# A hybrid gMLP and SSD streaming step on one core: the queues' order from the list schedule over the timeline model

## The chip, the cores and the metric

The kernel runs on one core of one Trainium2 chip. A core has five engines with a queue of instructions each: TensorE (PE, products), VectorE (DVE), ScalarE (ACT), GpSimd (POOL) and SyncE (SP, which here only issues DMAs). An engine takes its queue from the front; a semaphore makes it wait for another engine or for a DMA. The metric is the device time of one execution in microseconds (us), the median of several runs.

## The reference

One layer. The rows of a prompt of 4096 tokens and of a sample of 64 tokens are normalised, multiplied by one input projection, sent through two mixers and through one output projection:

```python
h = rms_norm(x, norm_in_w) @ w_in            # (tokens, 1024) @ (1024, 5648)
u, v, g, z, xbc, dt_raw = jnp.split(h, SPLITS, axis=-1)
a_out, vn = gmlp_branch(u, v, g, ...)        # (u * (W_s LN(v) + b)) * silu(g), chunks of 128
b_out, h_last, new_conv = mamba_branch(z, xbc, dt_raw, ...)  # conv, silu, SSD scan, norm(y * silu(z))
y = x + jnp.concatenate([a_out, b_out], axis=-1) @ w_out
y_prompt = rms_norm(yp, norm_f_w)
```

It returns both outputs, the final states of scan and convolution, and the normalised rows `vn` of the sample. All is float32.

## The kernel before, in words

**Number format.** A float32 operand of a large product is split into a high part (a cast to the format that TensorE takes, on ScalarE) and a low part (operand minus high part, on VectorE or GpSimd). Each product is then three: high by high, low by high, high by low. A matmul therefore waits for a cast and for a subtraction.

**Stages.** The 32 chunks of 128 tokens are cut into five blocks of 6 chunks and a last block of 2 chunks with the sample. For each block the rows are read, normalised and turned over (`xrows`: norm L481 on VectorE, transposes L488 on TensorE, copies L491 on ScalarE), and `right_operands` makes seven Strassen operands of them, called `hop1` to `hop7`: sums L524, L527, L530 and L533 (the second and third on VectorE, L533 on GpSimd), high parts L514 on ScalarE, low parts L515. Their products come in the order 1, 2, 4, 6, 7, 5, 3. The first columns of a block are the gMLP's values (`v_stage`, matmuls L1083 to L1085), the rest come by units of columns (`products`, matmuls L1123 to L1125, twelve for one weight tile). `add_up` (L1136 to L1153) adds the seven products out of PSUM. Convolution is at L1165 to L1186, the gate by z at L1223 to L1239 (its multiplication is `z_fin`, L1230 on VectorE).

**The weight operands.** In block 0 every weight operand is made on the chip, by `make`: sums of raw weights into `wx` tiles (L386, L401, L403, L405, mostly GpSimd), the cast L392 on ScalarE into a `w` tile, and the subtraction L393:

```python
src = r[{1: "a11", 2: "a12", 4: "a22", 6: "a11", 7: "a22", 5: "a21", 3: "a12"}[q]]
act.copy(hi, src)
(pool if q in self.on_pool[u[0]] else dve).tensor_tensor(lo, src, hi.bitcast(F32), SUB)
```

It is also stored to DRAM, and the later blocks load it from there (SP's queue). There are four `w` tiles; a load or a cast into one waits for the matmuls that read its contents before. The last block loads most operands and casts some (L358).

**The scan.** A unit of the scan is one chunk and one of two groups of heads. It loads running decay values (`acb`, DMA at L823), makes decays (`ssd_decay`, L864 to L869: two exponentials `ea` L869 on ScalarE), a masked matrix (`ssd_m`: eight L882 and one L885 on ScalarE, then L890 on VectorE), turns x over (L897) and scales it (`xdt` L907), multiplies (`ssd_y`: eight matmuls L928, four L931) and updates the state (L978 to L989). Units of one block are worked off between the products of the same block. ScalarE loads a table when the next function is not in the table that it holds; such loads stand in its queue as instructions of their own.

**Phase 2** multiplies the mixed rows by `w_out`: casts and subtractions L1582/L1583 for the weights and L1590/L1591 for the rows, matmuls L1628 to L1630, sums L1643/L1645, store L1650.

**What sets the order.** The source issues the instructions of all stages in one text order. The framework records them; at the end its list schedule makes the five queues: it keeps, for a modelled machine, when each engine is free and when each instruction's inputs are there, and puts next, of the instructions that are ready, the one that stood earliest in the text. An engine can so get later text first, wherever the model thinks that the earlier text is not ready. Order on a queue, semaphores, and the places of table loads follow from that.

## Time and profile before

| what | us |
|---|---|
| median of 3 runs | 2957.86 (2954.97 to 2960.79) |
| the profiled execution, its own time | 2957.03 |
| its span in the trace | 2955.1 |
| granted TensorE clock, mean | 0.982 of full speed |
| block 0 | 0 to 521 |
| blocks 1 to 4 | 521 to 2085, 391 each |
| last block and start of phase 2 | 2085 to 2320 |
| phase 2 | 2320 to 2955 |

The profile gives, for each engine, busy time and the idle time before its instructions with what ended it. Times in its rows are us from the start of the span unless marked ns. A line number names the place in the kernel's text. Tile names carry no number in the profile and carry one in the order of the instructions.

### The profile page before, as it was taken

What the parts mean: (1) busy time and instruction counts of PE and PEld (TensorE: products, weight loads), DVE (VectorE), ACT (ScalarE), POOL (GpSimd) and SP (SyncE); (2) the same over time, 40 slices, a digit from 0 to 9 for tenths busy, and PEclk for the clock granted to TensorE, in tenths of its full rate; (3) what the DMA queues carried; (4) which work ended last, traced back from release to release, by engine and by line L of the source; (5) the groups of instructions that cost most, each with busy time, mean ns of one, the idle gap of its engine ahead of it and who ended that gap; (6) DMA issues with size and microseconds to landing.
All of it is one profiled execution on the core that took longest, in us unless ns stands there. A gap on an engine that the chain in (4) does not pass through costs nothing. (4 is left out here: it accounts for less than half of the span.)

```text
span 2955.1 us, 46403 instructions
## 1 busy us (share of the span) xinstructions
PE 2826.3 (96%) x17159; PEld 2633.3 (89%) x17159; DVE 2162.7 (73%) x3607; ACT 1345.8 (46%) x2655; POOL 704.8 (24%) x575
## 2 busy tenths in 40 slices
PE   5988988999999999999999999999999899999998
PEld 5987887999999999999999999999899688878886
DVE  7888887667756777676677576874666766698887
ACT  4366655145643266541565514663365222253332
POOL 4554443110012100031000221000301433353332
PEclk8999998999999999999999999999999899999999
DMA  6666777777787777886777877778777555454553
GB/s 223 252 233 237 258 281 261 245 229 238 248 277 270 229 238 243 270 288 227 244 241 240 300 264 229 234 246 281 241 251 226 168 171 171 159 169 157 171 171 111
DMA packets 306809, 679.14 MB, mean 230 GB/s; under 512 B 30472, under 2 KB 154072, under 8 KB 306584
## 3 DMA queue, kind: packets, MB, share of 16 engines
q1 hardware_dynamic: 305544, 676.17, 68.6%
q8 instruction: 137, 2.24, 0.3%
q14 instruction: 88, 0.72, 0.1%
q10 hardware_dynamic: 1040, 0.00, 0.0%
HBM read 525.34 MB, written 150.75 MB: 229 GB/s over the span
## 5 line engine op out<-in xcount | busy, mean ns | idle before, releaser
L1123 PE MATMUL mm<-hop,w 128*128 128x384 f32 x1656 | 579.4, 350 | 7.1 <-ACT w L392 3.5
L1125 PE MATMUL mm<-hop,w 128*128 128x384 f32 x1656 | 564.9, 341 | 9.0 <-DVE w L393 4.5
L1124 PE MATMUL mm<-hop,w 128*128 128x384 f32 x1656 | 565.0, 341 | 0.0
L1629 PE MATMUL pa<-wlo,oh 128*128 128x512 f32 (+1 forms) x928 | 366.7, 395 | 13.0 <-DVE wlo L1583 13.0
L1630 PE MATMUL pa<-whi,ol 128*128 128x512 f32 (+1 forms) x928 | 364.9, 393 | 3.5 <-DVE ol L1591 3.5
L1628 PE MATMUL pa<-whi,oh 128*128 128x512 f32 (+1 forms) x928 | 365.2, 394 | 2.6 <-ACT whi L1582 1.4
L1123 PEld LDWEIGHTS mm<-hop,w 128*128 128x128 f32 x1656 | 315.4, 190 | 14.0 <-ACT w L392 7.0
L1125 PEld LDWEIGHTS mm<-hop,w 128*128 128x128 f32 x1656 | 315.3, 190 | 12.2 <-DVE w L393 7.0
L1124 PEld LDWEIGHTS mm<-hop,w 128*128 128x128 f32 x1656 | 315.5, 190 | 3.4 <-issue 2.4
L1123 PE MATMUL mm<-hop,wy 128*128 128x384 f32 x864 | 297.4, 344 | 0.0
L1125 PE MATMUL mm<-hop,wy 128*128 128x384 f32 x864 | 292.0, 338 | 0.0
L1124 PE MATMUL mm<-hop,wy 128*128 128x384 f32 x864 | 291.9, 338 | 0.0
L1629 PEld LDWEIGHTS pa<-wlo,oh 128*128 128x128 f32 (+1 forms) x928 | 174.6, 188 | 57.1 <-DVE wlo L1583 18.9
L1630 PEld LDWEIGHTS pa<-whi,ol 128*128 128x128 f32 (+1 forms) x928 | 174.8, 188 | 42.7 <-DVE ol L1591 4.2
L1628 PEld LDWEIGHTS pa<-whi,oh 128*128 128x128 f32 (+1 forms) x928 | 174.5, 188 | 42.5 <-ACT whi L1582 2.1
L123 POOL TENSOR_TENSOR rsx<-rsx,mhalf 128x1 f32<-128x1 f32 (+1 forms) x33 | 19.0, 588 | 736.6 <-DVE rsx L122 736.6
L1083 PE MATMUL mm<-w,hop 128*128 128x260 f32 x552 | 160.4, 291 | 16.2 <-ACT hop L514 16.2
L1085 PE MATMUL mm<-w,hop 128*128 128x260 f32 x552 | 159.6, 290 | 7.7 <-DVE hop L515 7.7
L882 ACT ACTIVATE acb<-acb,acu 128x128 f32<-128x128 f32 (+1 forms) x528 | 166.6, 389 | 0.6
L1124 PEld LDWEIGHTS mm<-hop,wy 128*128 128x128 f32 x864 | 162.6, 188 | 0.7
L1123 PEld LDWEIGHTS mm<-hop,wy 128*128 128x128 f32 x864 | 162.5, 188 | 0.8
L1125 PEld LDWEIGHTS mm<-hop,wy 128*128 128x128 f32 x864 | 162.3, 188 | 0.0
(333 smaller groups left out, 6517.8 us busy)
## 6 DMA issues: line engine op xcount, KB each, us to landing
w<-wop_c SPq DMA_DIRECT2D x114, 512.0 KB, 4.3
w<-wop_v SPq DMA_DIRECT2D x84, 520.0 KB, 5.0
w<-wop_u SPq DMA_DIRECT2D x76, 512.0 KB, 4.3
w<-wop_g SPq DMA_DIRECT2D x76, 512.0 KB, 4.4
w<-wop_z SPq DMA_DIRECT2D x76, 512.0 KB, 4.6
wy<-wop_c SPq DMA_DIRECT2D x72, 512.0 KB, 4.4
acb<-acd SPq DMA_DIRECT2D x66, 512.0 KB, 5.1
raw<-ab SPq DMA_DIRECT2D x64, 512.0 KB, 4.1
```

The source lines that it names most:

```text
L123: pool.tensor_tensor(out, out, mhalf[: out.shape[0]].to_broadcast(list(out.shape)), ALU.pow)
L882: act.activation(M[:L, i, :L], M[:L, i, :L], AF.Relu, bias=self.acu[:L, ci, h0 + i : h0 + i + 1])
L1083: pe.matmul(pv, a, hi[:, j, :], start=(j == 0), stop=False)
L1085: pe.matmul(pv, b, hi[:, j, :], start=False, stop=(j == 3))
L1123: pe.matmul(b, hi[:, j, :], thi[:, j, :], start=j == 0, stop=False)
L1124: pe.matmul(b, hi[:, j, :], tlo[:, j, :], start=False, stop=False)
L1125: pe.matmul(b, lo[:, j, :], thi[:, j, :], start=False, stop=j == 3)
L1628: pe.matmul(b, x[0][:, j, :], hi, start=first, stop=False)
L1629: pe.matmul(b, x[0][:, j, :], lo, start=False, stop=False)
L1630: pe.matmul(b, x[1][:, j, :], hi, start=False, stop=last)
```

## The change

One argument is added where the kernel's context is opened. The text of the kernel is the same, and so are its instructions, apart from ScalarE's table loads (116 in place of 106) and semaphores.

```diff
-    with _tile.TileContext(nc) as tc:
+    with _tile.TileContext(nc, schedule_with_timeline_sim=True) as tc:
         hybrid_step_kernel(tc, *args)
```

With it the list schedule goes by another machine model, the framework's timeline model, when it asks which instructions are ready. The rule, earliest text first, stays. On TensorE 11,583 of 15,979 instructions keep their place against the others, on VectorE 1,583 of 3,608, on ScalarE 1,006 of 2,485, on GpSimd 462 of 573. Three places show how.

ScalarE in block 0, before: `w_1812` to `w_1856` are weight operands, `ea_2265` belongs to unit 0 of the scan; the eight L882 of unit 0 come only behind these rows.

```order
L392 CAST w_1812<-wx_1449 128x512
L1186 ACT_TABLE_LOAD
L1186 ACTIVATE arena_155<-arena_155 128x768
L392 CAST w_1835<-wx_1627 128x512
L866 ACT_TABLE_LOAD
L866 ACTIVATE dte_2261<-dte_2261 128x16
L1186 ACT_TABLE_LOAD
L1186 ACTIVATE arena_155<-arena_155 128x768
L392 CAST w_1856<-wx_1816 128x512
L392 CAST w_1877<-wx_1816 128x512
```

The same place now; ahead of these rows stand already both L869 of units 0 and 1 (`ea_2265`, `ea_2354`) and the eight L882 of unit 0 (`acb_2252`).

```order
L866 ACTIVATE dte_2350<-dte_2350 128x16
L392 CAST w_1812<-wx_1449 128x512
L882 ACTIVATE acb_2259<-acb_2259,acu_311 128x128 x6
L392 CAST w_1835<-wx_1627 128x512
L882 ACTIVATE acb_2259<-acb_2259,acu_311 128x128 x2
L885 ACTIVATE acb_2252<-acb_2252 128x1024
L1186 ACT_TABLE_LOAD
L1186 ACTIVATE arena_155<-arena_155 128x768
L885 ACT_TABLE_LOAD
L885 ACTIVATE acb_2259<-acb_2259 128x1024
L848 COPY bt_2306<-ss_2254 128x256
L392 CAST w_1856<-wx_1816 128x512
```

The scan's exponentials and masks of two units now stand ahead of the casts `w_1812` to `w_1856`; before they stood behind them, in pieces.

TensorE in block 0, at the first L928; `hop6_151` and the like are the Strassen operands of the rows, `ss` and `mm` PSUM banks. Before:

```order
L1125 MATMUL mm_2358<-hop6_151,w_2222 128x384
L1123 MATMUL mm_2397<-hop7_152,w_2245 128x384
L928 MATMUL ss_2336<-acb_2252,xdt_2308 64x128 x8
L931 MATMUL ss_2345<-arena_155,S_147 128x128 x4
L897 MATMUL ss_2391<-ident_66,arena_155 128x128 x4
L1124 MATMUL mm_2397<-hop7_152,w_2245 128x384
L1125 MATMUL mm_2397<-hop7_152,w_2245 128x384
```

Now:

```order
L1125 MATMUL mm_2058<-hop3_154,w_1986 128x384
L928 MATMUL ss_2336<-acb_2252,xdt_2308 64x128 x8
L931 MATMUL ss_2345<-arena_155,S_147 128x128 x4
L1123 MATMUL mm_2080<-hop1_148,w_2007 128x384
L1124 MATMUL mm_2080<-hop1_148,w_2007 128x384
L1123 MATMUL mm_2101<-hop2_149,w_2028 128x384
L1124 MATMUL mm_2101<-hop2_149,w_2028 128x384
L1125 MATMUL mm_2080<-hop1_148,w_2007 128x384
```

Before, the scan's first products stood behind the products with `w_2222`; now they stand behind those with `w_1986`, eleven weight operands earlier, and the four L897 that followed them stand elsewhere. The products with `hop1` and `hop2` are interleaved at their start.

VectorE between two blocks (here from block 1 to block 2): L1230 is the gate of the old block, L515, L527 and L530 make the Strassen operands of the new one. Before:

```order
L1230 TENSOR_TENSOR arena_155<-arena_155 128x768
L1150 TENSOR_TENSOR arena_155<-mm_8751,arena_155 128x3x128
L1151 TENSOR_TENSOR arena_155<-mm_8751,arena_155 128x3x128
L515 TENSOR_TENSOR hop5_153<-t1_8475,hop5_153 128x768
L527 TENSOR_TENSOR arena_155<-arena_155,t1_8475 128x2x384
L527 TENSOR_TENSOR arena_155<-arena_155,t1_8476 128x2x384
L1153 TENSOR_TENSOR arena_155<-mm_8779,arena_155 128x3x128
L1153 TENSOR_TENSOR arena_155<-mm_8800,arena_155 128x3x128
L515 TENSOR_TENSOR hop4_150<-arena_155,hop4_150 128x768
L515 TENSOR_TENSOR hop6_151<-arena_155,hop6_151 128x768
```

Now:

```order
L515 TENSOR_TENSOR hop5_153<-t1_8475,hop5_153 128x768
L515 TENSOR_TENSOR hop5_153<-t1_8476,hop5_153 128x768
L1153 TENSOR_TENSOR arena_155<-mm_8779,arena_155 128x3x128
L1230 TENSOR_TENSOR arena_155<-arena_155 128x768
L1153 TENSOR_TENSOR arena_155<-mm_8800,arena_155 128x3x128
L1230 TENSOR_TENSOR arena_155<-arena_155 128x768
L527 TENSOR_TENSOR arena_155<-arena_155,t1_8475 128x2x384
L530 TENSOR_TENSOR arena_155<-arena_155 128x2x384
L527 TENSOR_TENSOR arena_155<-arena_155,t1_8476 128x2x384
L530 TENSOR_TENSOR arena_155<-arena_155 128x2x384
L1230 TENSOR_TENSOR arena_155<-arena_155 128x768
L515 TENSOR_TENSOR hop3_154<-arena_155,hop3_154 128x768 x2
```

Two L1230 and the second L515 of `hop5` now stand ahead of the first L527; L515 of `hop4`, which stood right behind L527 and L1153, now comes after `hop3`, `hop6` and half of `hop7`. The same move recurs at each of the later boundaries.

## Rows read from the trace of the kernel before

**Rows 1.** the page's first part: engine, busy us, share of the span, instructions

```profile
PE 2826.3 (96%) x17159; PEld 2633.3 (89%) x17159; DVE 2162.7 (73%) x3607; ACT 1345.8 (46%) x2655; POOL 704.8 (24%) x575
```

**Rows 2.** busy time by stretch: length, engines, granted clock, DMA share, GB/s

```profile
0.00:521.00 521.00, 440.22 (x2696) 415.44 (x2696) 424.26 (x632) 290.28 (x563) 251.45 (x187) 0.93 0.71 249
521.00:912.00 391.00, 385.44 (x2545) 375.96 (x2546) 270.91 (x482) 184.04 (x378) 36.39 (x45) 0.99 0.76 250
2085.00:2320.00 235.00, 218.48 (x1442) 200.98 (x1440) 157.63 (x366) 121.67 (x254) 55.13 (x38) 0.96 0.73 236
2320.00:2955.00 635.00, 615.79 (x2684) 500.39 (x2682) 489.28 (x670) 198.41 (x346) 226.99 (x167) 0.99 0.48 159
176.00:264.00 88.00, 74.38 (x403) 68.45 (x401) 70.47 (x87) 58.29 (x99) 50.55 (x43) 0.92 0.68 239
```

**Rows 3.** TensorE's waits in block 0: us in total, times, longest

```profile
PE mm L1083 <- ACT hop L514: 16.2, 2, 15.0
PE ss L928 <- issue: 10.9, 3, 4.9
...
PE ss L488 <- DVE xt L481: 7.7, 4, 4.0
PE ss L928 <- DVE acb L890: 5.3, 2, 4.7
```

**Rows 4.** TensorE's waits in the stretch 176 to 264 us alone

```profile
PE ss L928 <- issue: 4.2, 1, 4.2
PE mm L1125 <- POOL w L393: 4.0, 2, 3.6
PE mm L1123 <- ACT w L392: 2.6, 2, 1.7
```

**Rows 5.** groups on ScalarE, 176 to 264 us: busy, mean ns | idle before

```profile
L392 ACT CAST w<-wx 128x512 fp32r<-128x512 f32 x28 | 16.5, 612 | 15.9 <-POOL wx L405 12.6 <-DMA wx<-in_w_in_dram 1.2 <-POOL wx L401 1.1
L882 ACT ACTIVATE acb<-acb,acu 128x128 f32<-128x128 f32 x22 | 7.4, 392 | 0.1
...
L869 ACT ACTIVATE ea<-acb 64x512 f32<-64x512 f32 x6 | 3.8, 629 | 1.7 <-DVE arena L970 1.1 <-DMA acb<-acd 0.6
...
L885 ACT ACT_TABLE_LOAD x2 | 2.6, 1283 | 0.0
L885 ACT ACTIVATE acb<-acb 128x1024 f32<-128x1024 f32 x2 | 2.1, 1057 | 0.0
```

**Rows 6.** TensorE's waits in blocks 1 to 4 and the last block's start

```profile
PE ss L488 <- DVE xt L481: 7.5, 10, 1.6
```

**Rows 7.** VectorE in order of time, block 1 to 2: start, us, operation

```profile
902.76 0.95 DVE L1230 TENSOR_TENSOR arena<-arena 128x768 f32<-128x768 f32 x1
...
905.43 1.82 DVE L527 TENSOR_TENSOR arena<-arena,t 128x768 f32<-128x768 f32 x2
...
909.85 4.46 DVE L515 TENSOR_TENSOR hop<-arena,hop 128x768 fp32r<-128x768 f32 x4 [1.40 <-ACT hop L514]
914.23 1.81 DVE L530 TENSOR_TENSOR arena<-arena 128x768 f32<-128x768 f32 x2
```

**Rows 8.** TensorE in order of time: the third value product begins

```profile
916.38 0.28 PE L1083 MATMUL mm<-w,hop 128*128 128x260 f32 x1
```

**Rows 9.** groups on ScalarE in the last block, 2140 to 2245 us

```profile
L358 ACT CAST w<-wa 128x512 fp32r<-128x512 f32 x12 | 7.4, 613 | 7.4 <-issue 6.6 <-PE mm L1405 0.7
...
L1417 ACT COPY cvr<-mm 128x256 f32<-128x256 f32 (+1 forms) x16 | 3.8, 292 | 4.1 <-PE mm L1405 4.1
```

**Rows 10.** TensorE's waits in the same stretch of the last block

```profile
PE mm L1403 <- DMA w<-wop_c: 1.4, 1, 1.4
```

**Rows 11.** TensorE's waits in phase 2, 2320 us to the end

```profile
PE pa L1629 <- DVE wlo L1583: 5.9, 5, 2.3
PE pa L1630 <- DVE ol L1591: 3.5, 1, 3.5
```

## Prediction

> **What bounds the kernel now.** I read the page's first part, then the busy times by stretch, then TensorE's waits stretch by stretch. TensorE is busy 96% of the span [rows 1]: 2826.3 of 2955.1 us, so 129 us are idle. A new order of the same instructions can win nothing but idle time and slow clock. The stretches [rows 2] say where that is. Blocks 1 to 4 are nearly full (385.4 of 391 us in block 1). Block 0 is not: it lasts 521 us, TensorE is busy 440.2 of them, and the granted clock is 0.93. It does the work of a later block and makes the weight operands besides; VectorE is busy 424.3 us there, ScalarE 290.3, GpSimd 251.5. So 81 of the 129 idle us lie in block 0, 16.5 in the last block and the start of phase 2, 19.2 in phase 2, and some 12 in all of blocks 1 to 4. The forecast is therefore mostly one on block 0.
>
> TensorE's waits in block 0 [rows 3] are four kinds that count: 15.0 us once for the cast L514 of the fourth operand at the start, 10.9 and 5.3 us for the scan's products L928, and 7.7 us for the transposes L488. The rest are waits for weights, of a few us each. In the stretch 176 to 264 us [rows 4] the weights' part (4.0 for the low part, 2.6 for the cast) stands beside one L928 wait of 4.2 us. A wait of this length costs more than itself: in the 5 us behind that one the granted clock is 0.50 in the last line of [rows 2], the lower of the two levels, 1.2 GHz, so 5.0 us are spent on 2.5 us of work.
>
> The sum is made against the profiled execution, 2957.0 us with a span of 2955.1; the median of the runs is 2957.9, 0.9 us above, which I neglect.
>
> **Block 0, 176 to 264 us.** ScalarE's order puts the exponentials and masks of the scan's first two units ahead of the casts from `w_1812` on. Newly ahead of `w_1856` stand three L869 at 629 ns, sixteen L882 at 392, two L885 at 1057 and one table load at 1283 [rows 5]: 1.9 + 6.3 + 2.1 + 1.3 = 11.6 us. ScalarE's casts stand idle 15.9 us in the 88 us of this stretch, mostly until GpSimd's sums L405 are made [rows 5]; about a fifth of that, 2.8 us, lies ahead of `w_1856`, and takes up so much. The cast then comes some 8.8 us later, and queued behind it are the next casts, the evacuations L1136 and L1175 of the convolution, and through them VectorE's subtractions L393. TensorE, which had the cast just in time before, would wait up to 8.8 us. But a wait here lets GpSimd and VectorE run ahead, so that the later waits of 4.0 and 2.6 us [rows 4] are covered by it: net +2.2 us, to which I add 1.5 for the slower clock behind a longer wait, about +3.7. On the other side, TensorE's first L928 stand eleven weight operands earlier, and their inputs are ready by then: the 4.2 us wait and the 2.5 us lost at half clock behind it go, −6.7. Sum −3. The bounds: −13 if all three waits of rows 4 go with the slow clock (4.2 + 4.0 + 2.6 + 2.5), +9 if the 8.8 us stay whole and nothing is covered.
>
> On the table loads, rows 5 show 1283 ns each, and no idle time between a load and the L885 behind it (0.0). The Trainium skill, "ScalarE: Activation LUTs", section "What ACT_TABLE_LOAD costs", has about 1380 ns of drain on top, 2.66 us for a switch. By the page the ten loads more would put 27 us on ScalarE in place of 12.8, and the four ahead of `w_1856` would make it 5.5 us later still; the row decides, and shows no drain.
>
> The ten loads by the row are 12.8 us on an engine that is busy 46% [rows 1]. They cost nothing of their own where ScalarE waits anyhow; where it doesn't, they are in the 11.6 us above.
>
> **Later in block 0.** Of the other L928 waits 12.0 us are left (10.9 + 5.3 − 4.2, three long ones). In the new order some six matmuls of a product stand ahead of them; in the stretch 247 to 252 us thirty matmuls take 5.0 us at half clock [rows 2], so six take 0.5 us at full clock and 1.0 at half. Three times 1.0: −3 (0 to −12, the latter if VectorE's L890 comes early as well). The transposes L488 stand 36 to 47 matmuls later, that is 3 to 8 us by the same rate, against a longest wait of 4.0 [rows 3]. What would be late next is L491 and, behind it, the operands of block 1, which have no wait of their own before. I take −5 of the 7.7 (0 to −7.7).
>
> **Start of block 0.** L514 of `hop4` stands behind those of `hop7`, `hop5` and `hop6` in both orders, so the 15.0 us [rows 3] stay. Two casts of weights stand newly ahead of it, 0.6 us each by rows 5, and the normalisations of later rows come earlier on VectorE: 0, between −2 and +2.
>
> **Blocks 1 to 4.** Two things move against each other. The L488 waits, 7.5 us in ten places [rows 6], shrink as in block 0, since the transposes stand later: −5. At the boundary VectorE's two gates L1230 and a split of `hop5` now stand ahead of the first L527. One L1230 takes 0.95, an L527 0.91 (two in 1.82), a split 1.1 (four in 4.46) [rows 7]: the sums for `hop4` start three times about 0.95 later, and wait for ScalarE's gate besides; splits of `hop3`, `hop6` and `hop7` go ahead of that of `hop4`, some 4.5 to 5.5 us more. Before, the splits of `hop4` and `hop6` ended at 914.3 (909.85 + 4.46), and the third product began at 916.4 [rows 8]: 2.1 us of cover. TensorE takes the sixth and seventh operands ahead of the rest of the fourth now, each product about 4 us long, which makes up for most of the later split. Left is a wait of about 1.4 us, four times: +5.6 (0 to +7 each if no other product covers, that is +28 at the most). Together about +0.5.
>
> In the fourth convolution unit of each block two L869 and four L882 stand ahead of an evacuation: 2 × 0.63 + 4 × 0.39 = 2.8 us later [rows 5]. PSUM has three further banks, so TensorE feels only what is over: 0 to 2.8, I take 0.5, four times: +2.
>
> **Last block.** Two units of the scan stand ahead of casts L358 (12 of 613 ns) and evacuations L1417 (16 of 292 ns) [rows 9]; each unit is 2 L869, 8 L882, 1 L885 and a table load, 6.7 us by rows 5. TensorE waits only 1.4 us in this stretch [rows 10], so its cover is unknown. Bounds: 0, and the 13.4 us of both units. The casts show 7.4 us of idle time before them, so half of 13.4 is taken up, and a part by banks: +3.
>
> **Phase 2.** The steady part has the same order on TensorE. The 3.5 us wait on L1591 [rows 11] has its row split ahead of a weight's now; the 5.9 us on L1583 stay. −1 (−4 to +3).
>
> **Sum.** −3 −3 −5 +0 +0.5 +2 +3 −1 = −6.5; 2957.0 − 6.5 = 2950.5, say 2951.
>
> **The rivals.**
> *Weights starve TensorE in block 0 (slower).* The place is ScalarE's queue from `w_1812` on. For it: the casts were just in time, ScalarE is busy 58.3 of the 88 us, VectorE 70.5, GpSimd 50.6 [rows 2], so a delay is made good slowly; and the pattern returns with the other units. Against it: 12.6 us of the casts' idle time were spent on GpSimd, which the scan's work on ScalarE could fill. Price: 8.8 us whole, some 4 us at each of three later pairs of units, and 2.5 us of slow clock behind each of the four: 8.8 + 12 + 10 = +31; less the −11 of the other terms, about +20: 2977. It decides where the delay per pair of units is over 5 us.
>
> The Trainium skill, "PSUM — Partial Sum Buffer", section "Engine vs sequencer instructions", calls ScalarE's queue a strict FIFO: no ready cast passes a unit of the scan, which is what this rival needs; of the size of the delay it says nothing.
>
> *Block 0 gains as a whole (faster by more).* If scan products and transposes are ready wherever they now stand, all of 16.2 us (L928) and 7.7 (L488) go, with 2.5 us of slow clock behind each of the three longest: −31, less +8 for the last block, the boundaries and the units: about 2934. For it: TensorE idles 81 us in block 0. Against it: VectorE is busy 81% of the block, and what L928 waits for passes through it.
>
> *Nothing moves in time.* If VectorE sets block 0's pace, the waits only change their names: 2957, ±4. For it: 424 of 521 us busy. Blocks 1 to 4 have no more than 12 us to give or lose before. That the switch does nothing at all is excluded by the order.
>
> **How the numbers follow.** Forecast 0.40 (2943 to 2958), starved weights 0.24 (2967 to 2987), larger gain 0.18 (2925 to 2943), nothing 0.18. A measurement of this kernel can tell about 0.2%, 6 us, from no change; the forecast's 6.5 us lies at that edge, so it splits: 0.23 faster, 0.15 same, 0.02 slower. With the larger gain, faster is 0.41; same 0.15 + 0.16 = 0.31; slower 0.24 + 0.02 + 0.02 = 0.28. The forecast's own range is 2943 to 2958. The range that leaves out 2 in 10 takes in most of both other cases: 2928 to 2982.
>
> **What would show it.** Right: TensorE's waits for L928 in block 0 fall from 16.2 us to about 9, those for L488 in blocks 0 to 4 from 15 to about 5; waits for `w` L392/L393 between 176 and 264 us grow by 2 to 4 us; block 0 ends 8 to 14 us earlier, and the later blocks are no shorter. Wrong: block 0 ends later than 521 us with waits for `w` over 20 us; or a wait for L515 of `hop4` or `hop6` of over 3 us at each boundary; or a wait for L358 or L1417 of over 8 us in the last block.

## The result, and the profile after

The changed kernel takes 3003.41 us (median of 4 runs, 3000.88 to 3007.13) against 2956.41 us for the kernel before in the same comparison: a ratio of 1.0158, with a 95% interval of 1.0140 to 1.0175. It is slower by 47 us. The prediction was 2951 us, with its widest range from 2928 to 2982; the result lies above all of them. The profiled execution has a span of 3005.4 us and a mean granted clock of 0.979.

The first part of the page of the changed kernel, in the columns of [rows 1]:

```profile
PE 2843.8 (95%) x17159; PEld 2636.7 (88%) x17159; DVE 2185.3 (73%) x3607; ACT 1359.5 (45%) x2665; POOL 718.4 (24%) x575
```

TensorE is busy 17 us longer, and its idle time has grown from 129 to 162 us. Some 9 of the 17 us go with the mean granted clock, 0.979 in place of 0.982 (an estimate: 2826.3 us times their ratio).

Busy time by stretch, as in [rows 2]; the first seven lines are block 0, blocks 1 to 4, the last block with the start of phase 2, and phase 2, each cut where the same instructions stand as in the kernel before, and the last line is the stretch of block 0 on which the prediction rested:

```profile
0.00:531.00 531.00, 440.43 (x2704) 408.60 (x2704) 443.77 (x636) 292.55 (x570) 259.41 (x188) 0.94 0.71 249
531.00:927.00 396.00, 389.93 (x2573) 380.72 (x2573) 269.89 (x486) 185.57 (x379) 36.81 (x42) 0.99 0.75 246
927.00:1324.00 397.00, 390.65 (x2575) 381.67 (x2576) 273.51 (x485) 188.36 (x383) 47.61 (x49) 0.99 0.75 248
1324.00:1729.00 405.00, 394.84 (x2604) 384.96 (x2602) 281.36 (x489) 192.68 (x388) 55.06 (x54) 0.99 0.76 248
1729.00:2127.00 398.00, 392.38 (x2585) 382.52 (x2585) 262.55 (x480) 172.56 (x344) 35.86 (x42) 0.99 0.73 239
2127.00:2374.00 247.00, 222.58 (x1445) 201.66 (x1444) 162.26 (x372) 122.61 (x255) 52.67 (x36) 0.97 0.68 221
2374.00:3005.00 631.00, 612.95 (x2680) 496.58 (x2678) 491.98 (x664) 205.19 (x347) 231.00 (x169) 0.99 0.49 160
176.00:264.00 88.00, 71.00 (x369) 65.21 (x369) 72.49 (x84) 57.16 (x98) 48.45 (x38) 0.92 0.60 210
```

Block 0 has grown by 10 us, blocks 1 to 4 by 5, 6, 14 and 7, the last block's stretch by 12; phase 2 got 4 back. Blocks 1 to 4, of which the prediction said that they had no more than 12 us to give or lose, have lost the most.

TensorE's waits over the whole of the changed kernel (us in total, times, longest), to be held against [rows 3, 6, 10, 11]:

```profile
PE mm L1083 <- ACT hop L514: 27.8, 5, 19.8
PE mm L1125 <- DVE w L393: 15.3, 11, 4.2
PE mm L1123 <- DVE cvr L1153: 13.7, 4, 3.5
...
PE mm L1123 <- ACT w L392: 8.3, 6, 4.2
...
PE ss L488 <- DVE xt L481: 7.4, 4, 2.5
PE mm L1403 <- DMA w<-wop_u: 6.5, 4, 2.5
PE mm L1083 <- DVE arena L1138: 6.1, 2, 3.4
PE pst L978 <- DVE xdt L944: 5.9, 3, 3.5
```

The long waits for L928 (16.2 us in block 0) are all but gone, as are those of L488 in blocks 1 to 4. In their place stand four waits of L1123 for L1153 and two of L1083 for L1138, which the kernel before did not have at all, more waits for weights (L393, L392), and longer ones for L514 at the start and the block boundaries.

**Where the time went, counted on the same instructions.** Since the instructions are the same, each of TensorE's can be looked up in both traces. The table gives the median of (start after minus start before) for those that started within 4 us of the named time in the kernel before, and cuts the span at 640, 860, 1030, 1250, 1420, 1640, 1812, 2037, 2320 us, and 2940 near the end. "Block 0" is all up to 640 us, with the boundary behind it. "Units" is the sum of the four differences 640 to 860, 1030 to 1250, 1420 to 1640 and 1812 to 2037, which hold the fourth convolution unit of each block and a part of the block's middle; "boundaries" is what lies between these.

| run | block 0 | units | boundaries | last block | phase 2 | at the end |
|---|---|---|---|---|---|---|
| the change | 10.4 | 22.1 | 9.4 | 12.1 | -3.8 | 50.2 |
| units_back | 8.7 | -1.7 | 7.8 | 10.4 | -4.8 | 20.4 |
| l1175_first | 9.7 | 7.8 | 12.4 | 13.3 | -5.2 | 38.0 |
| l1175_early | 10.3 | -0.7 | 16.2 | 13.3 | -6.4 | 32.7 |
| bounds_back | 10.6 | 16.4 | 6.3 | 13.6 | -3.3 | 43.6 |
| l533_dve | 5.8 | 19.5 | 20.5 | 11.7 | -3.7 | 53.8 |
| block0_back | 3.1 | 21.1 | 10.0 | 9.2 | -6.0 | 37.4 |
| block0_act_back | -2.6 | 22.1 | 5.6 | 8.3 | -5.6 | 27.8 |
| last_back | 9.6 | 18.3 | 9.1 | 1.9 | -1.2 | 37.7 |
| last_act_back | 7.5 | 19.8 | 5.8 | 9.2 | -3.1 | 39.2 |
| last_sp_back | 10.0 | 20.1 | 11.0 | 7.7 | 0.6 | 49.4 |
| last_actsp_back | 7.8 | 22.6 | 13.9 | 1.7 | 0.5 | 46.5 |
| last_rest_back | 8.5 | 18.3 | 9.1 | 19.5 | -1.2 | 54.2 |
| most_back | 2.4 | -1.4 | 5.5 | -0.9 | 0.4 | 5.9 |
| units_only | -0.6 | 7.3 | -0.3 | 5.6 | -1.7 | 10.3 |
| units_act_alone | 2.6 | 24.2 | -0.6 | 1.5 | -0.5 | 27.2 |
| gains | -8.9 | -0.9 | 6.3 | 4.1 | -2.1 | -1.5 |
| gains_b0 | -9.0 | 0.2 | 0.0 | 1.3 | -2.4 | -9.9 |
| gains_b0act | -4.2 | 1.1 | -1.5 | 3.9 | -1.6 | -2.3 |

At 860, 1250 and 1640 us the shift is not steady: in the changed kernel it falls from 15.3 us at 830 to 10.3 at 912, from 22.7 at 1200 to 17.7 at 1303 and from 30.3 at 1560 to 26.8 at 1697. Cut where it is steady and where both kernels have started the same matmuls, by line, tiles and count (518, 640, 830, 912, 1030, 1200, 1303, 1420, 1560, 1697, 1812 and 2037 us), the same traces give:

| run | block 0 to 518 | first boundary | units | middles | three boundaries |
|---|---|---|---|---|---|
| the change | 3.0 | 7.5 | 27.9 | -13.5 | 17.0 |
| units_back | 1.7 | 7.3 | 4.0 | -13.4 | 15.5 |
| l1175_first | 2.5 | 7.3 | 13.7 | -13.6 | 20.1 |
| l1175_early | 2.9 | 7.5 | 5.1 | -13.4 | 23.8 |
| bounds_back | 3.3 | 7.7 | 22.4 | 0.0 | 0.4 |
| l533_dve | 0.6 | 5.7 | 25.4 | -13.5 | 28.2 |
| block0_back | 3.1 | -0.1 | 27.0 | -13.4 | 17.5 |
| block0_act_back | -5.6 | 3.5 | 28.2 | -13.6 | 13.0 |
| last_act_back | 1.6 | 6.1 | 25.7 | -13.5 | 13.4 |
| last_actsp_back | 1.7 | 6.2 | 28.5 | -13.6 | 21.6 |
| most_back | 2.7 | 0.2 | 4.2 | -0.2 | 0.0 |
| units_act_alone | 2.3 | 0.2 | 23.3 | -0.5 | 0.8 |
| gains | -7.3 | -1.5 | 4.8 | 0.7 | 0.0 |
| gains_b0 | -5.9 | -3.0 | -0.2 | -0.1 | 0.5 |

The new order gains 13.5 us in the stretches ahead of the three boundaries, in every run that has it there, and pays 13 to 24 us at the boundaries. One middle in both kernels, with the same 447 matmuls:

```profile
830.00:909.30 79.30, 75.96 (x447) 73.51 (x447) 43.20 (x72) 39.61 (x89) 15.88 (x14) 1.00 0.89 297
```

```profile
845.30:919.60 74.30, 74.30 (x447) 73.74 (x446) 42.70 (x73) 39.65 (x89) 13.27 (x11) 1.00 0.91 316
```

One trace has noise. Between runs with the same order in a stretch, block 0 in the first table came out between 5.8 and 10.6 us, the units of the second between 22.4 and 28.5, the three boundaries between 13.0 and 23.8 (in the first table 5.6 to 16.2), and last block and phase 2 together between 2.7 and 10.3.

**The fourth convolution unit, the largest part.** ScalarE in order of time, in block 1 of the changed kernel (start, us, operation, idle time before it and what ended it):

```profile
642.63 1.28 ACT L869 ACT_TABLE_LOAD   x1
648.46 1.29 ACT L869 ACTIVATE ea<-acb 64x512 f32<-64x512 f32 x2 [4.55 <-DMA acb<-acd]
...
663.92 1.28 ACT L885 ACT_TABLE_LOAD   x1
665.22 1.06 ACT L885 ACTIVATE acb<-acb 128x1024 f32<-128x1024 f32 x1
666.18 1.01 ACT L1175 ACTIVATE arena<-cvr,prm 128x768 f32<-128x768 f32 x1
```

VectorE and TensorE behind it:

```profile
667.29 1.02 DVE L1178 SCALAR_TENSOR_TENSOR arena<-cvr,prm,arena 128x768 f32<-128x768 f32 x1 [9.21 <-ACT arena L1175]
668.23 0.55 DVE L1153 TENSOR_TENSOR cvr<-mm,cvr 128x384 f32<-128x384 f32 x1
```

```profile
668.84 0.44 PE L1123 MATMUL mm<-hop,w 128*128 128x384 f32 x1 [3.40 <-DVE cvr L1153]
```

The chain is read backwards. TensorE's L1123 stands still for 3.40 us, because the PSUM bank it writes to is freed by L1153 on VectorE. L1153 is ready; it stands in VectorE's queue behind L1178, and L1178 waits 9.21 us for ScalarE's L1175. L1175 in turn is ready, but stands in ScalarE's queue behind two units of the scan: a table load at 642.63, then 4.55 us of nothing until the unit's `acb` has come by DMA, then L869, L882 and L885 of both units up to 666.18. In the kernel before, the same L1178 and L1153:

```profile
649.07 1.02 DVE L1178 SCALAR_TENSOR_TENSOR arena<-cvr,prm,arena 128x768 f32<-128x768 f32 x1 [1.47 <-ACT arena L1175]
650.00 0.55 DVE L1153 TENSOR_TENSOR cvr<-mm,cvr 128x384 f32<-128x384 f32 x1
```

There L1178 waited 1.47 us, and TensorE did not wait. The same happens four times, and costs more than the wait where the clock falls behind it:

```profile
668.00:673.00 5.00, 4.17 (x23) 4.17 (x24) 4.96 (x7) 3.52 (x4) 1.73 (x2) 1.00 0.26 67
1065.00:1070.00 5.00, 5.00 (x17) 5.00 (x17) 4.88 (x7) 3.17 (x5) 1.10 (x3) 0.50 0.16 26
```

In block 1 the granted clock stayed at 1.00 behind the wait of 3.40 us, and the shift grew by 3.7 us from 640 to 680 us; in block 2, behind a wait of 3.3 us, it is 0.50 for the next five (1.2 GHz), and the shift grew by 6.2 us from 1030 to 1070. In block 3, behind a wait of 3.5 us, the clock is 0.57 over 1465 to 1470, in block 4 it is 0.83 over 1867 to 1872.

### The profile page after: what moved, and what is told of

Its sections match the earlier page's. It is cut to its first block, busy times and chain, and to the rows that moved or that the text cites. A ratio compares the mean times of both kernels' runs of the same rounds, so it can differ in the third digit from the quotient of the medians.

```text
span 3005.4 us, 46472 instructions
## 1 busy us (share of the span) xinstructions
PE 2843.8 (95%) x17159; PEld 2636.7 (88%) x17159; DVE 2185.3 (73%) x3607; ACT 1359.5 (45%) x2665; POOL 718.4 (24%) x575
## 4 chain that ended last, share of the span: by engine, by line
PE 72%; DVE 10%; ACT 7%; DMA 6%; issue 4%; POOL 1%; SPq 1%; POOLq 0%; ACTq 0%; DVEq 0%
PE mm L1123 11%; PE mm L1125 11%; PE mm L1124 11%; PE pa L1630 6%; PE pa L1629 6%; PE pa L1628 6%; PE mm L1085 2%; PE ss L931 2%; PE ss L928 2%; PE mm L1084 2%; PE mm L1083 2%; ACT acb L882 2%; PE ss L761 2%; DMA wx<-in_w_in_dram 1%; DMA acb<-acd 1%
## 5 line engine op out<-in xcount | busy, mean ns | idle before, releaser
L1123 PE MATMUL mm<-hop,w 128*128 128x384 f32 x1656 | 580.1, 350 | 28.0 <-DVE cvr L1153 13.7
L1125 PE MATMUL mm<-hop,w 128*128 128x384 f32 x1656 | 567.1, 344 | 17.8 <-DVE w L393 15.3
L1123 PEld LDWEIGHTS mm<-hop,w 128*128 128x128 f32 x1656 | 316.2, 191 | 37.2 <-DVE cvr L1153 15.0
L1123 PE MATMUL mm<-hop,wy 128*128 128x384 f32 x864 | 296.8, 344 | 0.6 <-ACT cvr L1136 0.6
L123 POOL TENSOR_TENSOR rsx<-rsx,mhalf 128x1 f32<-128x1 f32 (+1 forms) x33 | 21.1, 640 | 752.2 <-DVE rsx L122 751.1
L1083 PE MATMUL mm<-w,hop 128*128 128x260 f32 x552 | 162.4, 297 | 33.9 <-ACT hop L514 27.8
L1123 PEld LDWEIGHTS mm<-hop,wy 128*128 128x128 f32 x864 | 162.9, 188 | 1.7 <-ACT cvr L1136 0.9
L1085 PE MATMUL mm<-w,hop 128*128 128x260 f32 x552 | 159.1, 292 | 5.3 <-DVE hop L515 5.3
L882 ACT ACTIVATE acb<-acb,acu 128x128 f32<-128x128 f32 (+1 forms) x528 | 162.9, 387 | 0.8
```

The source lines that it names most:

```text
L882: act.activation(M[:L, i, :L], M[:L, i, :L], AF.Relu, bias=self.acu[:L, ci, h0 + i : h0 + i + 1])
L1083: pe.matmul(pv, a, hi[:, j, :], start=(j == 0), stop=False)
L1085: pe.matmul(pv, b, hi[:, j, :], start=False, stop=(j == 3))
L1123: pe.matmul(b, hi[:, j, :], thi[:, j, :], start=j == 0, stop=False)
L1125: pe.matmul(b, lo[:, j, :], thi[:, j, :], start=False, stop=j == 3)
```

## The experiments

All of them are the kernel before or the changed one, with the order of some instructions laid down. No instruction is added or left out, apart from ScalarE's table loads; only l533_dve moves some to another engine. `PIN` is a list of rows of instruction numbers; each row's instructions are put in this order on their engine, without a wait:

```diff
         hybrid_step_kernel(tc, *args)
+        seen = {i.name: i for i in nc.cur_bb.bb.instructions}
+        first = _mybir.DependencyInfo(_mybir.DependencyClass.NoSync, _mybir.DependencyReason.DATA)
+        for row in PIN:
+            for a, b in zip(row, row[1:]):
+                tc.add_manual_dep(seen[f"I-{b}"], f"I-{a}", first, reason="pin")
```

The list schedule still makes the rest of the queues, so an order laid down on one engine can move instructions on others. Ratios are to the kernel before in the same comparison, with their 95% intervals.

### The convolution units

**units_back.** `PIN`: on ScalarE, 36 instructions around each fourth convolution unit, in the order of before, in the changed kernel.

> The changed kernel with one thing undone: in blocks 1 to 4, ScalarE's order of 36 instructions around the fourth convolution unit is put back to the one before (by order-only edges); all else stays. The trace of the changed kernel loses 4.8, 7.9, 8.2 and 7.0 us in these four places, counted on TensorE's instructions against the kernel before. Theory A (ScalarE's scan work ahead of L1175 holds VectorE's L1178, L1153 behind it holds the PSUM bank): the time falls by 20 to 28 us, to about 2978. Rival B (the blocks' pace is set elsewhere, and a wait taken away here comes back in the same block): it falls by less than 8 us, and the waits of L1123 for L1153 (13.7 us) turn up under another name.

Measured: 2979.61 us, ratio 1.0089 (1.0071 to 1.0107) against 1.0158. That is 0.69%, 20 us, and the four units cost nearly nothing any more (first table: 22.1 to -1.7; second: 27.9 to 4.0). No wait of L1123 for L1153 is left. Theory A holds, B falls: the other parts of the tables stay within their noise.

**units_only.** The kernel before, with the changed order of these 36 instructions, four times.

> The kernel before with one thing done: the same four stretches of ScalarE's queue in the changed kernel's order; the list schedule goes by the plain model for the rest. Theory A: TensorE waits in the fourth convolution unit of each block, 5 to 7 us each, 20 to 28 us in all, to about 2980. Rival B: within 6 us of the kernel before.

Measured: 2967.88 us, ratio 1.0041 (1.0026 to 1.0056). Slower, but the units cost 7.3 us in place of the 20 to 28 expected. The reason is in VectorE's order of time, which the list schedule had made again around the new ScalarE order:

```profile
648.35 0.56 DVE L1153 TENSOR_TENSOR cvr<-mm,cvr 128x384 f32<-128x384 f32 x1 [1.10 <-PE mm L1125]
656.53 1.95 DVE L1178 SCALAR_TENSOR_TENSOR arena<-cvr,prm,arena 128x768 f32<-128x768 f32 x2 [7.62 <-ACT arena L1175]
```

L1178 waits 7.62 us for L1175 here too, but L1153 now stands ahead of it and frees the bank in time. ScalarE's order is half of the cause only. The 5.6 us in the last block, of which 1.7 come back in phase 2, are noise of one trace, not a changed order: by lines and tiles every queue there stands as in the kernel before.

**units_act_alone.** To separate the two, all queues of the kernel before are laid down as they were, ScalarE's with the four stretches exchanged.

> The kernel before with the queues of TensorE, VectorE, GpSimd and SyncE held exactly as they were, and ScalarE's 36 instructions at the four convolution units in the changed kernel's order; unlike in the run units_only, VectorE's queue is not made again around it. Theory A (it takes both orders: L1175 late on ScalarE, and L1153, which frees the PSUM bank, behind L1178 on VectorE): 4 to 8 us for each unit, 16 to 32 us in all, to about 2979. Rival C (the new ScalarE order costs what units_only showed, 1.5 us for each unit, and the rest of the changed kernel's loss there comes from other queues): about 6 us, to 2962.

Measured: 2981.37 us, ratio 1.0076 (1.0058 to 1.0094). The table has 24.2 us for the units and nothing much elsewhere. TensorE's waits in blocks 1 to 4:

```profile
PE mm L1123 <- DVE cvr L1153: 12.7, 4, 3.4
```

This is the changed kernel's wait (13.7 us), made in the kernel before by ScalarE's order alone, while VectorE has L1153 behind L1178. Together the two runs show that it takes both.

**l1175_first.** Rows of two: the L1175 that L1178 waits for, ahead of the L885 of the scan's first unit, in the changed kernel.

```diff
+PIN = [[6228, 6494], [10260, 10526], [14292, 14558], [18324, 18590]]
```

> The changed kernel with one order-only edge for each of the four units: the L1175 that VectorE's L1178 waits for goes ahead of the L885 of the scan's first unit. The evacuation L1136 stays as late as the changed kernel has it. Theory A (the wait runs by L1175, L1178, L1153): most of the units' loss goes, the time falls by 15 to 25 us, to 2978 to 2988. Rival D (as the prediction had it, the evacuation L1136 and its bank set the wait): less than 5 us.

Measured: 2996.37 us, ratio 1.0132 (1.0114 to 1.0151). A weak edit: the list schedule answered by moving the L885 behind, and L1175 came only 1.5 us earlier (664.61 in place of 666.18). L1178 waited 8.3 us in place of 9.21. Even so the wait in block 1 shrank from 3.40 to 2.5 us, all four from 13.7 to 8.4, and the units' share from 22.1 to 7.8 (second table: 27.9 to 13.7): the price goes with how late L1175 is. Behind the 2.5 us in block 1 the clock stayed at 1.00.

**l1175_early.** The same with more edges: the first L1175 ahead of the first L885 and the second unit's first L882, the second L1175 and its evacuation ahead of the rest.

> The changed kernel with order-only edges on ScalarE in the four units, stronger than in l1175_first: the first L1175 goes ahead of the first unit's L885 and the second unit's first L882, the second L1175 and its evacuation ahead of the rest. ScalarE's early L869 and its wait for the acb DMA (4.6 us) stay as they are. Theory A: VectorE's wait for L1175 (9.2 us) falls to under 3, L1123's wait for L1153 goes, the time falls by 18 to 28 us, to about 2980, as with units_back. Rival D' (the wait for the acb DMA at the head is what costs): less than 10 us.

Measured: 2985.99 us, ratio 1.0083 (1.0061 to 1.0104). The units cost -0.7 us, though ScalarE still waits 4.50 us for the `acb` at the head: rival D' falls, and with it the wait for the DMA as the direct cause. L1175 now starts at 661.57. No wait of L1123 for L1153 is left in blocks 1 to 4. The longest in total there is now at the boundaries:

```profile
PE mm L1083 <- DVE arena L1138: 12.8, 4, 3.4
```

It was 6.1 us, and the boundaries have risen from 9.4 to 16.2 (second table: 17.0 to 23.8), so part of the gain is spent there, though their order is not changed. What sets their price with one order is seen below, at l533_dve.

### Block 0

**block0_back.** All five queues of block 0 in the order of before, in the changed kernel.

> The changed kernel with the order of block 0 (all that began in the first 535 us of the kernel before, on all five queues) put back to the one before. The traces differ by 10.4 us at the end of block 0. Theory A (stages add up): the time falls by 8 to 13 us, to about 2993, and block 0 ends at 521 again. Rival B (a faster block 0 only meets later transfers and waits): less than 4 us.

Measured: 2990.91 us, ratio 1.0118 (1.0094 to 1.0141), 0.40% or 12 us less than the change; block 0 ends 7.3 us earlier, and the other parts stand. By the second table all of it is at the first boundary (7.5 to -0.1), which this run puts back too. The 3.1 us that are left ahead of it arise between 285 and 450 us, where the old order is laid down, and units_act_alone and most_back, with the same old order there, have 2.3 and 2.7: noise, it seems, of the traces compared, not a rest of the new order. The stages add up.

**block0_act_back.** On ScalarE alone, what began in 172 to 264 us is put back.

> The changed kernel with ScalarE's order alone put back in block 0 for what began between 172 and 264 us in the kernel before; the other queues are made again around it by the same list schedule. Theory F (the casts behind the scan's exponentials cost place A: weight waits grew from 7 to 16 us there): TensorE's waits for w in this stretch fall back to about 7, block 0 ends 4 to 8 us earlier, the time falls by 4 to 8 us. Rival G (weights in block 0 are bound by GpSimd's sums and by VectorE, and the wait turns up later): less than 2 us.

Measured: 2991.95 us, ratio 1.0107 (1.0088 to 1.0126), 0.51% or 15 us less. TensorE's waits between 176 and 264 us in the changed kernel, and in this run:

```profile
PE mm L1125 <- DVE w L393: 8.2, 4, 4.2
PE mm L1123 <- ACT w L392: 6.7, 3, 4.2
PE mm L1125 <- POOL w L393: 1.4, 2, 1.1
```

```profile
PE mm L1125 <- DVE w L393: 4.3, 2, 3.3
PE mm L1123 <- ACT cvr L1136: 2.9, 1, 2.9
PE mm L1123 <- ACT w L392: 1.3, 3, 0.6
```

The weights' waits were 16.3 us and are 5.6. Block 0 now ends 2.6 us before that of the kernel before: ScalarE's order at this one place, with what the schedule makes of the other queues behind it, cost 13 us (10.4 to -2.6; the noise of block 0 is 5 us), and the rest of the new order is, over the whole of block 0, better than the old. Theory F holds, and more than it said.

### The boundaries

**bounds_back.** All five queues in 90 us around each of the three boundaries between blocks 1 to 4 put back.

> The changed kernel with the three boundaries between blocks 1 to 4 (what began in the 90 us around each in the kernel before, on all five queues) put back. Theory A (L1230 and the other splits ahead of L527 and of the split of hop4): the waits of L1083 for L514 and L1138 at these places go, L533 on GpSimd takes 1.8 to 2.6 us again in place of up to 6.8, and the time falls by 3 to 8 us, to 2995 to 3000. Rival B (the boundary's wait only stands for one that comes later anyway): less than 2 us.

Measured: 2998.48 us, ratio 1.0135 (1.0120 to 1.0150), 0.23% or 7 us less. The intervals of this ratio and of the change's, 1.0158, overlap. The traces are clearer: at the three boundaries TensorE's waits of L1083 and L1085 for L514, L515 and L1138 fall from 9.3 us to none, and the second table has 0.4 us there in place of 17.0. But the 13.5 us gained just ahead are gone too: the waits for L488 are back (9.7 us). So the order that moves the transposes back and the sums of the next block forward wins ahead of the boundary what it pays behind it, in net 3.5 us in the trace of the change and -0.6 to 10.4 in others with the same order. L533 is back at 1.84 to 2.5 us.

**l533_dve.** On GpSimd the trace of the changed kernel has L533 at this boundary as follows:

```profile
920.94 6.82 POOL L533 TENSOR_TENSOR arena<-arena 128x768 f32<-128x768 f32 x1 [22.25 <-DVE arena L527]
...
928.59 1.84 POOL L533 TENSOR_TENSOR arena<-arena 128x768 f32<-128x768 f32 x1
```

6.82 us for the first, 1.84 for the same operation 8 us later. The run moves the eight L533 of the boundaries to VectorE and holds the other queues.

```diff
-                (dve if start else pool).tensor_tensor(b21[:, sl[i]], b21[:, sl[i]], b11[:, sl[i]], SUB)
+                dve.tensor_tensor(b21[:, sl[i]], b21[:, sl[i]], b11[:, sl[i]], SUB)
```

> The changed kernel with the queues of TensorE, ScalarE and SyncE held, and the eight sums L533 of the block boundaries moved from GpSimd into VectorE's queue, right behind the sums that they wait for. On GpSimd the trace has them at 1.83, 2.5 or 6.82 us, the last beside a train of VectorE's sums and splits. Theory K (GpSimd is kept out by that train): they take 0.95 us each on VectorE, the cast of hop4 starts 4 to 5 us earlier at two boundaries, and those boundaries cost 1 to 2 us less each; the whole falls by 2 to 8 us. Rival L (VectorE's own queue sets the split of hop4, cast or not): no less, or 1 us more for each boundary.

Measured: 3011.45 us, ratio 1.0174 (1.0161 to 1.0188): no faster, and the boundaries cost 20.5 us in place of 9.4. TensorE's waits in blocks 1 to 4 say why:

```profile
PE mm L1083 <- DVE arena L1138: 23.3, 4, 6.7
```

L1138 empties a PSUM bank on VectorE; its wait was 6.1 us. VectorE and GpSimd at the first of these boundaries, in this run:

```profile
920.55 2.61 DVE L1230 TENSOR_TENSOR arena<-arena 128x768 f32<-128x768 f32 x1
...
925.60 2.55 DVE L533 TENSOR_TENSOR arena<-arena 128x768 f32<-128x768 f32 x1
```

```profile
920.10 4.76 POOL L1239 TENSOR_TENSOR ssum<-ssum,arena 128x768 f32<-128x768 f32 x2 [0.28 <-ACT arena L1232]
```

GpSimd, freed of L533, runs its four L1239 here, the first 3.9 us behind VectorE's first L527, where in the changed kernel it was 11.3. Beside them four operations of VectorE, one L533 among them, take 2.55 to 2.61 us each in place of 0.95, and the first L1138 starts 14.3 us behind the first L527, where it was 6.1. The same stands at the two later boundaries. So the 28.2 us are not the price of two L533 in VectorE's queue, which at 0.95 each would be 1.9 us of the 8.3 a boundary: the rest is what VectorE lost beside GpSimd.

Whether the long L533 is what a boundary costs is answered by the changed kernel itself. At its third boundary L533 took 2.51 us on GpSimd, with VectorE beside it:

```profile
1717.78 2.51 POOL L533 TENSOR_TENSOR arena<-arena 128x768 f32<-128x768 f32 x1 [21.81 <-DVE arena L527]
```

```profile
1718.48 2.62 DVE L527 TENSOR_TENSOR arena<-arena,t 128x768 f32<-128x768 f32 x1
...
1721.89 2.61 DVE L1230 TENSOR_TENSOR arena<-arena 128x768 f32<-128x768 f32 x1
```

That boundary cost 8.1 us, and TensorE waited 3.4 for L1138; the two with an L533 of 6.82 cost 4.5 and 4.4, and TensorE did not wait for L1138. In the eleven traces with this order, every one of the 11 boundaries with L533 at 2.5 us has a wait of 3.3 to 3.4 us for L1138 and costs 7.7 to 8.1, and every one of the 22 with an L533 of 6.8 us has none and costs 4.2 to 6.5. So theory K falls, and the other way round: where GpSimd is kept out, VectorE keeps its pace and L1138 comes in time; where GpSimd gets in, VectorE's operations are the long ones, L1138 is late, and TensorE waits. This is most of the noise of the boundaries.

### The last block

**last_back, last_act_back, last_sp_back, last_actsp_back, last_rest_back.** What began between 2080 and 2330 us (for last_act_back 2130 to 2300) in the order of before, in the changed kernel: on all five queues, on ScalarE, on SyncE, on both, and on the other three.

> The changed kernel with the order of the last block and the start of phase 2 (all that began between 2080 and 2330 us in the kernel before, on all five queues) put back. The traces differ by 9.0 us over this stretch. Theory A (stages add up): the time falls by 6 to 11 us, to about 2995, and TensorE's waits L1403 for the DMA of its weights (6.5 us) go back to 1.4. Rival B (the loads come late because of what stood ahead of them in block 4): less than 3 us, and the waits L1403 stay.

> The changed kernel with ScalarE's order alone put back in the last block for what began between 2130 and 2300 us in the kernel before. Theory F (casts L358 and evacuations behind L869, which waits 13.5 us for its DMA there): the loss of this stretch, 8 to 12 us in the trace, goes for the most part, the time falls by 5 to 10 us. Rival G (the loads on SyncE's queue behind stores, 6.5 us of L1403 waiting for w): less than 3 us, and those waits stay.

> The changed kernel with SyncE's order alone put back for what began between 2080 and 2330 us in the kernel before (last block). ScalarE's order alone had taken back some 2 us of the 8 to 12 that the traces lose there, all five queues together nearly all. Theory G (weight loads L417 and L420 stand behind stores that wait for late work): TensorE's waits for w by DMA (L1374, L1375, L1403, 12 us in the changed kernel) fall to about 6, the stretch loses 4 to 8 us less, the time falls by 4 to 8 us. Rival J (it takes the late casts and the late stores together): less than 3 us.

> The changed kernel with ScalarE's and SyncE's orders put back in the last block (what began between 2080 and 2330 us in the kernel before); TensorE, VectorE and GpSimd are made again around them. ScalarE's alone gave back about 2 of the 8 us of this stretch, SyncE's alone none, all five nearly all. Rival J (late casts and late stores together): the stretch loses under 3 us, the time falls by 4 to 8 us. Theory M (TensorE's and VectorE's own order of the last block costs it): the stretch still loses over 5 us.

> The opposite: TensorE's, VectorE's and GpSimd's orders put back in the same stretch, ScalarE and SyncE made again around them. Theory M: the stretch loses under 3 us, the time falls by 4 to 8 us. Rival J: it still loses over 5 us.

Measured: ratios 1.0147 (1.0130 to 1.0163), 1.0120 (1.0102 to 1.0139), 1.0162 (1.0148 to 1.0176), 1.0117 (1.0098 to 1.0137) and 1.0170 (1.0155 to 1.0186), against 1.0158 (1.0140 to 1.0175). In the first table last block and phase 2 belong together, since phase 2 takes some of the delay up. Their sum is 8.3 us in the changed kernel, and 0.7, 6.1, 8.3, 2.2 and 18.3 in the five runs; runs with the changed kernel's order there have 2.7 to 10.3.

The two witnesses agree on two points: SyncE's order alone brings nothing back, nor do the other three engines' (18.3 is outside the noise: they are worse without ScalarE's and SyncE's). On ScalarE they differ. By the ratios its order alone is worth 0.38%, as much as with SyncE's, 0.41%; by the traces it is worth 2 us, within the noise, and only both together, or all five, go below it, the former just so. The time of last_back fell by 3 us only, not by 6 to 11, though TensorE's waits L1403 for its weights went from 6.5 to 1.7 us, as expected. So ScalarE's order is part of the loss; whether SyncE's has to go with it (rival J) is not shown. In the changed kernel, ScalarE waits in this stretch as follows:

```profile
ACT L869 <- DMA acb<-acd: 13.4, 3, 8.5
```

In the kernel before it was 5.6 us. Table loads and L869 stand waiting for `acb`, ahead of casts and evacuations, as in the units. On SyncE, stores (L1440) wait for late work, 25.9 us in place of 11.1, and weight loads stand behind them; the largest waits there are the loads' own, L420 for TensorE to have read a `w` tile (39.5 us, before 35.1).

### Is there a better order?

**most_back.** Block 0, the units on ScalarE, the three boundaries and the last block to 2300 us put back in the changed kernel; the new order stays in the middles and in phase 2.

> The changed kernel with block 0, the four units on ScalarE, the three boundaries and the last block up to 2300 us all put back; the new order is left in the middles of the blocks and in phase 2. Theory A (the stages add up): 2951 to 2960, equal to the kernel before or a little faster, since phase 2 gained 0.7 us. Rival E (the parts overlap, and the rest of the new order costs time too): over 2965.

Measured: 2963.46 us, ratio 1.0014 (1.0005 to 1.0024). Between the two expectations: nearly all of the loss is in the named places. What stays new brings nothing but costs some 4 us: the second table has 4.0 us in the units' stretches in units_back, 4.2 here and 4.8 in gains, where ScalarE's 36 instructions have the old order and the rest of these stretches the new one in whole or in part.

**gains.** The kernel before, with the changed order where the shift fell: 70 to 172 us, 425 to 500 us and the middles of blocks 1 to 4.

> The kernel before with the changed kernel's order in the stretches where the traces show it ahead of the kernel before: 70 to 172 us (2.5 us), 425 to 500 us (3.9 us) and the middles of blocks 1 to 4 (about 1 us each); all else held as before, on all queues. If these are gains of their own: 2947 to 2952, 0.2 to 0.35% faster. Rival H (they are time given back after a delay that the new order made just ahead of them): 2955 to 2960, no difference.

Measured: 2951.11 us, ratio 0.9977 (0.9967 to 0.9986). Block 0 ends 8.9 us earlier. The first table puts 6.3 us of what is given back at the boundaries, by its cuts; by the second it is inside the blocks, 4.8 and 0.7 us, and none at the boundaries. Last block and phase 2 add 2.0, within their noise.

**gains_b0.** The same without the middles.

> The kernel before with the changed kernel's order only in 70 to 172 us and 425 to 500 us, without the middles of the blocks, all other queues held. The run gains was 9.0 us ahead at the end of block 0, and gave 5 to 7 back at the later boundaries and in the last block. If the middles did that: 2946 to 2951, 0.2 to 0.35% faster than the kernel before. Rival H (the later blocks give it back whatever the middles do): 2953 or more.

Measured: 2947.34 us, ratio 0.9959 (0.9946 to 0.9971): 0.41% or 12 us faster than the kernel before, the fastest of all. The 9.0 us gained in block 0 last to the end, so rival H falls: without the middles, the 5 us that the run gains lost in them stay won. Busy time in the two stretches, in the kernel before and in this run:

```profile
70.00:172.00 102.00, 95.69 (x655) 92.54 (x655) 88.24 (x164) 34.05 (x51) 52.39 (x42) 0.98 0.69 247
425.00:521.00 96.00, 78.89 (x435) 75.47 (x433) 68.67 (x90) 51.65 (x111) 36.38 (x24) 0.91 0.77 275
```

```profile
70.00:172.00 102.00, 97.71 (x670) 95.50 (x670) 89.55 (x165) 35.35 (x53) 53.63 (x44) 0.98 0.70 249
425.00:521.00 96.00, 81.86 (x474) 78.74 (x474) 79.02 (x101) 57.56 (x121) 40.92 (x25) 0.93 0.80 287
```

TensorE is busy 97.71 us in place of 95.69 in the first and 81.86 in place of 78.89 in the second, and VectorE 79.02 in place of 68.67 there: the same work is done sooner.

**gains_b0act.** The kernel before, with block 0 from 70 us on in the order that block0_act_back had.

> The kernel before with block 0 from 70 us on in the order of the run block0_act_back (the timeline model's order, with ScalarE's casts of 172 to 264 us kept ahead of the scan), the start and all later stages held as before. That run's trace made up 6 us from 100 us to the end of block 0 against the kernel before. If stages add up: 2948 to 2953. Rival H: 2954 or more.

Measured: 2953.30 us, ratio 0.9981 (0.9971 to 0.9991). Faster, with 4.2 us less in block 0 in place of the 6 expected, and 3.9 lost again in the last block, where nothing was changed; 1.6 of them come back in phase 2, and runs with the old order there have -1.1 to 3.9 for both together.

## Why the prediction was wrong, step by step

**The step that failed: "PSUM has three further banks, so TensorE feels only what is over: 0 to 2.8, I take 0.5, four times: +2."** The place was named and the sign was right, but the units cost 20 us by the ratios and 22.1 by the first table (27.9 by the second), ten times the term and twice its upper bound (11). Two things were wrong in it. The delay was put at 2.8 us, two L869 and four L882, from a count of what stands ahead of one evacuation. It left out that the L869 at the head waits 4.55 us for its DMA, that five table loads come between, and above all that the next L1175 stands behind both units: L1178 waited 9.21 us. And the price was sought on the engine that was moved, at the evacuation L1136. It was paid by way of VectorE, whose L1178 waits in order for L1175 while L1153 behind it holds the bank. That VectorE has instructions queued behind a waiting one was asked for block 0's casts and not here.

The miss of this term is 18 of the 54 us between forecast and result. Block 0's is as large, 21: its terms gave -11, and up to 640 us it lost 10.4. Boundaries with middles and the last block make up the rest.

**Block 0, 176 to 264 us: forecast -3, measured +3.8** (shift from 1.7 to 5.5). The count was right: `w_1856` was to come 8.8 us later. ScalarE in the changed kernel (six of the second unit's eight L882, then three casts from `w_1856` on), and the same cast before:

```profile
190.19 1.86 ACT L882 ACTIVATE acb<-acb,acu 128x128 f32<-128x128 f32 x6
...
198.78 1.66 ACT L392 CAST w<-wx 128x512 fp32r<-128x512 f32 x3
```

```profile
187.96 1.14 ACT L392 CAST w<-wx 128x512 fp32r<-128x512 f32 x2 [1.21 <-DMA wx<-in_w_in_dram]
```

198.78 less 187.96 is 10.8, of which 1.7 is the general shift: 9.1 us. The L928 wait went, as forecast. What failed is "a wait here lets GpSimd and VectorE run ahead, so that the later waits of 4.0 and 2.6 us [rows 4] are covered by it": the weights' waits rose from 7.1 to 16.3 us, so nothing was covered; for the waits the bound, "the 8.8 us stay whole", was the value. block0_act_back shows that this order cost more in the end, 13 us. The half clock that the prediction counts behind the 4.2 us wait stands in this line of the kernel before, which [rows 2] do not have:

```profile
247.00:252.00 5.00, 5.00 (x30) 4.67 (x29) 4.49 (x5) 1.83 (x4) 0.81 (x1) 0.50 0.70 209
```

Two slips of the working change little: a fifth of 15.9 us is 3.2, not 2.8, and the waits of L928 leave out 1.7 us for L907.

**Later in block 0: forecast -3 and -5, measured +5 to the first boundary's end** (5.5 to 10.4), and not in one piece: the shift is 14.4 us at 400, 8.3 at 505, 3.0 at 518 and 10.4 at 534. From 505 to 518 the waits of L1083 and L1084 for `wy` (3.2 us) went; the 7.4 behind it are the first boundary. L928's waits fell from 16.2 us (17.9 with L907) to 0.4 (L890) and 3.3 (L907), more than forecast; the L488 waits in block 0 did not fall, 7.7 to 7.4 us. In their place came L978 waiting for L944 (5.9 us) and L1123 for L1147 (4.3 us), which the working did not have. **The rival "block 0 gains as a whole" was half right:** gains_b0 shows 9.0 us of gain in two stretches, once ScalarE's order at 172 to 264 us is not taken along. Of the signs of being wrong, the first came: block 0 ended at 531 us with 28 us of waits for `w`. The other two, L515 and L358 or L1417, did not.

**Start: forecast 0, measured +4.2**, of which 2.5 come back by 170 us; L1083 waited 19.8 us for L514 where it had waited 15.0. The bound was 2.

**Boundaries: forecast +5.6, measured 7.4 at the end of block 0 and 17.0 over the three others,** four times the term, near the bound of 28. What the working had wrong is the cover: the sixth and seventh operands do not make up for the later split, and L1138, the evacuation that stands behind the same sums on VectorE (6.1 of the 18.1 us of waits there), is not in it. **The counterpart, -5 for the L488 waits of blocks 1 to 4, measured -13.5** in the three middles: those waits went from 9.8 us to none, and TensorE, busy 75.96 of 79.30 us in one of them, is busy throughout. Both terms were too small; their sum, forecast +0.5, is +3.5 without the first boundary and within the noise of the boundaries.

**Last block: forecast +3, measured 12.1, of which 3.8 come back in phase 2.** The bound of 13.4 held. The forecast had looked at ScalarE alone; how much SyncE's order adds stays open.

**Table loads: right.** They stand at 1283 ns each, and L885 starts 0.02 us after its load (663.92 + 1.28, and 665.22 in the lines above): the drain of the Trainium skill's page "ScalarE: Activation LUTs", section "What ACT_TABLE_LOAD costs", shows in neither kernel.

**The chances.** The rival that ended on the other side named block 0 as the place of the loss, at +20. Block 0 lost 10 us with its boundary, and stood for a fifth of the loss. No rival was about blocks 1 to 4, because they had little idle time to lose; that was the error of method. Here the nearly full stretches lost 32 us and the idle one 10: a delay in them comes once for each block, and there was little idle time to take it up.

## What to carry to other kernels

When a new order puts work ahead of an instruction on an in-order engine, follow the chain to the third engine: who waits for the late instruction, and what stands behind that one in its queue, above all the operation that empties a PSUM bank. Price a moved group by all that stands ahead of the late instruction, with table loads and with the DMA that its first one waits for, and price the full stretches first, times the number of their repeats. A schedule as a whole can be worse while parts of it are better: taken by stretches, the order that cost 1.6% gave one that is 0.4% faster than the kernel before. And cut a comparison of two traces only where the shift is steady: a cut on a slope puts a gain and a loss into the wrong columns.

## What the runs showed of the hardware

The same L533 on GpSimd took 1.84, 2.5 or 6.82 us, by what VectorE did beside it: 6.82 while VectorE ran L527, L530, L1230 and L515, all of two operands, without a gap from 919.9 us on at 0.95 us each or less. It ends at 927.8, 1.8 us after VectorE's next operation with an operand in PSUM (L1138, at 925.99) has started, and 1.83 is the shortest L533 there is. At 2.5 us it is VectorE that is held: L527 and L1230 take 2.6 us in place of 0.95. The Trainium skill, page "SBUF — State Buffer", section "Summary: rules for kernel authors", says that of a VectorE operation with two SBUF inputs and a GpSimd operation that reads SBUF the second to issue is held until the first is done. The 2.5 and 2.6 us agree with that; the 6.82 do if several of VectorE's in a row count as one. Which of the two outcomes a boundary gets, with one order, is not shown; the one that looks worse on GpSimd was cheaper for TensorE by 3 us in the mean (4.9 against 7.9).

A wait of 3.40 us on TensorE left the granted clock at 1.00 in one block, and one of 3.3 us was followed by 0.50 in the next, with 2.5 us lost behind it. So the same stall can cost 3.7 us or 6.2, and the sum for four of them is uncertain by some 10 us, an estimate from these two; with the same order one unit cost between 4.0 and 8.4 us.

What stays open: what decides at a boundary whether GpSimd's L533 or VectorE comes first, how the loss of the last block divides between ScalarE and SyncE, and why the new order costs 1 us in each block's unit stretch even with the units put back.
